# Where the tiles of a two-layer decoder trunk lie in on-chip memory: every large tile moved to a multiple of 512 bytes

## The chip, the cores and the metric

The kernel runs on one core of a Trainium2 chip. The metric is device time in microseconds for one execution, the median of several runs. The profile shown is of one execution of its own.

## The reference

The kernel computes a two-layer trunk on 512 tokens of width 1024, in float32. Cut to what matters:

```python
for i in range(2):
    if i == 0: mix = ssd_mixer(h, ...)        # in_proj, causal conv, chunked scan, gate, out_proj
    else:      mix = mla_attention(h, ...)    # low-rank q, shared compressed k/v, softmax, out_proj
    h = layer_norm(DN_ALPHA * h + mix, ln_mix_g[i], ln_mix_b[i])
    u = causal_depthwise_conv(h @ ffn_up[i], ffn_conv_w[i], ffn_conv_b[i])    # 1024 -> 2 x 2816
    g, val = split(u)
    h = layer_norm(DN_ALPHA * h + (silu(g) * val) @ ffn_down[i], ln_ffn_g[i], ln_ffn_b[i])
    if i == 0: shared_kv = mla_shared_kv(h, ...)
```

## The kernel before

**Arithmetic.** Every large product is done three times over in the fast float32 matmul format (float32r). Each operand is split into a high part, rounded to that format, and the rest, the low part; the product is high by high, plus low by high, plus high by low. Two helpers issue them. `mm_a` (the matmul is L123) keeps a 128x128 piece of a weight tile in the array (`wh` is its high part, `wl` its low part) and streams 512 (sometimes 256) columns of a transposed activation tile past it, `ht` in most places and `cT` in the attention's head projections. `mm_b` (L129, L130, L131) does it the other way round: a 128x128 piece of an activation tile stays in the array (`gt` in the FFN's down projection, `yT` in the SSD output projection, `oT` in the attention output projection, `cT` and `ht` in the attention's first projections), and 512 columns of `wh` or `wl` stream. What stays is the stationary operand, loaded by its own LDWEIGHTS instruction; what streams is the moving operand. Each matmul has a load of its own.

**Weights.** `WStream` brings weight pieces of 128x1024 from memory by DMA on SyncE's queue into `wst` (3 buffers). ScalarE rounds them into `wh` (L60), VectorE subtracts into `wl` (L61), 6 buffers each.

**Stages.** They follow each other: `ssd` (to about 433 us), `ffn` with its up projection, convolution and down projection (to about 790 us), `mla` (to about 985 us), and `ffn` again, whose last row block ends in `ln_last`. Within a stage TensorE, VectorE and ScalarE work side by side, in the order in which the program is written.

**Where tiles lie.** Tiles come from pools. A pool takes its place in on-chip memory behind the pools opened before it that are still open, each tile's size rounded up to 32 bytes; a tile has the same byte address in all 128 partitions. Pools of the class `K` live throughout; those of a stage are closed with it, and the next stage uses the same bytes. Some 1 KiB of tiles of a few bytes or a few hundred bytes (`mhalf`, `posi`, `freq`, `posf` in the pool `const`, `lnst` and `lnlast` in `lns`, `cw4`, `rstd`, `ng`, `hb` at the front of the SSD's pool, `css` and `smx` in `a2` ahead of the pool of `oT`) stand between or ahead of the large ones and shift all that come behind. So the large tiles lie at odd places. The remainder of each large tile's address by 512 in the built program:

| tiles | what they are | remainder before |
|---|---|---|
| `wst`, `wh`, `wl`, `ht`, `h`, `lngb` | weights, transposed activations (also V in the attention), residual, norm gains | 352 |
| `gt`, `acc`, `cw` | FFN | 32 |
| `yT`, `cv`, `th`, `W`, `y` and the other SSD tiles | SSD | 160 |
| `cT`, `ka`, `kb`, `qT`, `kT`, `qrT`, `PT`, `E` | attention | 32 |
| `oT` | attention output | 224 |
| `warm`, `ident` | constants | 128 |

All slices that a matmul takes of these tiles step by whole multiples of 512 bytes, but for the 288-column pieces of the SSD's first projection (steps of 128) and one of the attention's first projection (a step of 256).

Of the kernel before, what the change touches and what calls it, by code (L numbers as in the profile page):

```python
# [9 lines left out]
F32 = mybir.dt.float32  # L10
F32R = mybir.dt.float32r
BF16 = mybir.dt.bfloat16
I32 = mybir.dt.int32
# [5 lines left out]
P = 128  # L19
SEQ = 512  # L20
NT = SEQ // P
# [9 lines left out]
class WStream:  # L31
    def __init__(self, k, items, nb, nst, la):
        self.k, self.items, self.nb, self.nst, self.la = k, items, nb, nst, la
        self.loaded = 0
        self.split = 0
        self.done = 0
        self.st = {}
        self.w = {}
# [44 lines left out]
class K:  # L83
    def __init__(self, tc, ctx, nb=6, nst=3, la=4):
        self.tc, self.nc, self.ctx = tc, tc.nc, ctx
        nc = self.nc
        self.nb, self.nst, self.la = nb, nst, la
        pool = lambda n, b, **kw: ctx.enter_context(tc.tile_pool(name=n, bufs=b, **kw))
        self.const = pool("const", 1)
        self.hp = pool("hp", 1)  # L90
        self.htp = pool("htp", 1)
        self.wst = pool("wst", nst)
        self.wh = pool("wh", nb)
        self.wl = pool("wl", nb)
        self.lnp = pool("lnp", 1)
        self.lns = pool("lns", 2)
        self.ps = pool("ps", 8, space=PSUM)
        self.warm = self.const.tile([P, P], F32, name="warm")
        nc.vector.memset(self.warm, 1.0)
        self.ident = self.const.tile([P, P], F32, name="ident")  # L100
        make_identity(nc, self.ident)
        self.mhalf = self.const.tile([P, 1], F32, name="mhalf")
        nc.gpsimd.memset(self.mhalf, -0.5)
        self.h = self.hp.tile([P, NT, DM], F32, name="h")
        self.pend = []
        self.st = {}
# [32 lines left out]
    def add_mix(self, i, hf, ps, scale, last=False):  # L139


        hs = self.h[:, i, hf * 512:(hf + 1) * 512]
        kw = {}
        if last:
            if i not in self.st:
                self.st[i] = self.lns.tile([P, 6], F32, name="lnst", bufs=4)
            kw["accum_out"] = self.st[i][:, hf:hf + 1]
        a, b = (hs, ps) if isinstance(scale, float) else (ps, hs)
        self.nc.vector.scalar_tensor_tensor(hs, a, scale, b, op0=ALU.mult, op1=ALU.add, **kw)  # L149
# [18 lines left out]
    def ln_last(self, i, bs, out):  # L168

        nc = self.nc
        hv = self.h[:, i, :]
        s = self.st.pop(i)
        t = self.lns.tile([P, 12], F32, name="lnlast", bufs=1)
        c, qa, qb, sb, nmu, d, q, v, e, rstd, sa = (t[:, j:j + 1] for j in range(11))
        junk = self.junk[0].tile([P, DM], BF16, name="lnjunk", tag=self.junk[1])
        h2, h3 = hv[:, 512:768], hv[:, 768:]
        nc.vector.scalar_tensor_tensor(h2, h2, 1.0, bs[0], op0=ALU.mult, op1=ALU.add, accum_out=sa)
        nc.vector.tensor_scalar(sa, sa, s[:, 0:1], None, op0=ALU.add)  # L180
        nc.vector.tensor_scalar(c, sa, -1.0 / 768, None, op0=ALU.mult)
        nc.scalar.activation(junk[:, :768], hv[:, :768], AF.Square, bias=c, accum_out=qa)
        nc.vector.scalar_tensor_tensor(h3, h3, 1.0, bs[1], op0=ALU.mult, op1=ALU.add, accum_out=sb)
        nc.vector.tensor_scalar(nmu, sb, sa, -1.0 / DM, op0=ALU.add, op1=ALU.mult)
        nc.scalar.activation(junk[:, 768:], h3, AF.Square, bias=c, accum_out=qb)
        nc.vector.tensor_scalar(d, nmu, c, None, op0=ALU.subtract)
        nc.gpsimd.tensor_scalar(q, qa, 1.0 / DM, LN_EPS, op0=ALU.mult, op1=ALU.add)
        nc.vector.tensor_scalar(e, d, d, q, op0=ALU.mult, op1=ALU.subtract)
        for sl in (slice(0, 512), slice(512, 1024)):
            nc.vector.scalar_tensor_tensor(hv[:, sl], hv[:, sl], nmu, self.gb[:, 0, sl], op0=ALU.add, op1=ALU.mult)  # L190
        nc.gpsimd.tensor_scalar(v, qb, 1.0 / DM, e, op0=ALU.mult, op1=ALU.subtract)
        nc.gpsimd.tensor_tensor(rstd, v, self.mhalf, op=ALU.pow)
        for sl in (slice(0, 512), slice(512, 768), slice(768, 1024)):
            nc.vector.scalar_tensor_tensor(hv[:, sl], hv[:, sl], rstd, self.gb[:, 1, sl], op0=ALU.mult, op1=ALU.add)
            nc.sync.dma_start(out[:, sl], hv[:, sl])
# [153 lines left out]
NH, HD, NG, HPG, NS = 32, 64, 8, 4, 128  # L349
# [27 lines left out]
def ssd(k, ws, base, xT, x, cwp, hv, ngp, gb):  # L377
    nc, tc = k.nc, k.tc
    with ExitStack() as cx:
        pool = lambda n, b, **kw: cx.enter_context(tc.tile_pool(name=n, bufs=b, **kw))  # L380
        one = pool("s1", 1)
        cvp = pool("cv", 8)
        thp = pool("th", 2)
        k.junk = (thp, "th")
        ytp = pool("yt", 7)
        drp = pool("drp", 1, space=DRAM)


        cw = one.tile([P, 32, 5], F32, name="cw4")
        rstd = one.tile([P, NG, NT], F32, name="rstd")  # L390
        ng = one.tile([P, 2, 16], F32, name="ng")
        hb = one.tile([P, 2, NH], F32, name="hb")
        ht = k.new_ht()
        tri = one.tile([P, P], F32, name="tri")
        nc.gpsimd.memset(tri, 1.0)
# [408 lines left out]
def rope_tables(k, pos, freq):  # L804

    nc = k.nc
    c = k.const
    N = NT * 32
    pi = c.tile([P, NT], I32, name="posi")
    nc.sync.dma_start(pi, pos)  # L810
    fr = c.tile([P, 32], F32, name="freq")
    nc.sync.dma_start(fr, freq.broadcast_to([P, 32]))
    pf = c.tile([P, NT], F32, name="posf")
    nc.vector.tensor_copy(pf, pi)
    cs = c.tile([P, 2, NT, 32], F32, name="cossin")
    t = c.tile([P, 2, N], F32, name="ropet")
    a, m = t[:, 0], t[:, 1]
    v = lambda x: x.rearrange("p (c f) -> p c f", c=NT)
    nc.vector.tensor_tensor(v(a), pf.unsqueeze(2).broadcast_to([P, NT, 32]), fr.unsqueeze(1).broadcast_to([P, NT, 32]), op=ALU.mult)
    nc.vector.tensor_scalar(m, a, float(1.0 / (2.0 * np.pi)), ROUND, op0=ALU.mult, op1=ALU.add)  # L820
    nc.vector.tensor_scalar(m, m, ROUND, None, op0=ALU.subtract)
    for w in (TWO_PI_HI, TWO_PI_MID, TWO_PI_LO):
        nc.vector.scalar_tensor_tensor(a, m, -float(w), a, op0=ALU.mult, op1=ALU.add)
    lim = float(np.float32(3.1415925))
    sn = cs[:, 1].rearrange("p c f -> p (c f)")
    co = cs[:, 0].rearrange("p c f -> p (c f)")
    nc.vector.tensor_scalar(sn, a, lim, -lim, op0=ALU.min, op1=ALU.max)
    nc.vector.tensor_scalar(co, a, float(np.pi / 2), None, op0=ALU.add)
    nc.vector.tensor_scalar(m, co, float(np.pi), -2.0 * float(np.pi), op0=ALU.is_gt, op1=ALU.mult)
    nc.vector.tensor_tensor(co, co, m, op=ALU.add)  # L830
    nc.vector.tensor_scalar(co, co, lim, -lim, op0=ALU.min, op1=ALU.max)
    csf = cs.rearrange("p a c f -> p (a c f)")
    nc.scalar.activation(csf, csf, AF.Sin)
    k.cs = cs
# [18 lines left out]
def mla(k, ws, base, ngp, gb):  # L853
    nc, tc = k.nc, k.tc
    with ExitStack() as cx:
        pool = lambda n, b, **kw: cx.enter_context(tc.tile_pool(name=n, bufs=b, **kw))
        one = pool("a1", 1)
        two = pool("a2", 2)
        otp = pool("ot", 7)
        k.junk = (one, "E3")  # L860
        ng = one.tile([P, QR + KVR], F32, name="ang", tag="E3")
        nc.sync.dma_start(ng, ngp.broadcast_to([P, QR + KVR]))
# [246 lines left out]
def trunk_kernel(tc, *aps):  # L1109
    d = dict(zip(_INS, aps))  # L1110
    out = aps[len(_INS)]
    with ExitStack() as ctx:
        ctx.enter_context(tc.manual_schedule(engines={mybir.EngineType.SP}))
        k = K(tc, ctx)
        items = ssd_items(d['xbc'], d['zdt'], d['zw'], d['sow'])
        items += ffn_items(d['up'][0], d['down'][0])
        items += mla_items(d['dw'], d['vw'], d['rw'], d['hw'], d['aow'])
        items += ffn_items(d['up'][1], d['down'][1])
        ws = WStream(k, items, k.nb, k.nst, k.la)
        n = ssd(k, ws, 0, d['xT'], d['x'], d['cw4'], d['hv'], d['sng'], d['gb'][0])  # L1120
        rope_tables(k, d['pos'], d['freq'])
        n = ffn(k, ws, n, d['cw3'][0], d['gb'][1], la=5)
        n = mla(k, ws, n, d['ang'], d['gb'][2])
        n = ffn(k, ws, n, d['cw3'][1], d['gb'][3], out=out)
# [53 lines left out]
```

## Time and profile before

| what | value |
|---|---|
| median of 3 runs | 1360.01 us (1358.56 to 1360.58) |
| the profiled execution's own time | 1358.62 us |
| its span, first to last instruction | 1356.9 us |
| granted TensorE clock, share of full speed | 0.998 |
| TensorE matmul (PE) busy | 1341.7 us, 99% of the span |
| weight loads (PEld), overlapping PE | 1127.2 us, 83% |
| VectorE (DVE), ScalarE (ACT), GpSimd (POOL) busy | 885.6, 585.6, 71.5 us |
| mean traffic with memory | 100 GB/s |

In the profile PE is the matmul and PEld the weight load. A matmul's recorded duration holds its way through the array too, so that matmuls which follow each other overlap in the record: what one costs is the distance from its start to the next one's start. That distance is called the pace below. It is read from the timeline, which gives start times, or from the chain of work, which gives the length of an unbroken run of matmuls and their count.

### The profile page before, as it was taken

To read this page: it belongs to the slowest core of one execution; us is meant where nothing else is said; L and a number is where in the kernel's file an instruction comes from. 1 tells how busy PE (TensorE), PEld (TensorE's weight loads), DVE (VectorE), ACT (ScalarE), POOL (GpSimd) and SP (SyncE) were. 2 spreads that over 40 slices of the span, in tenths; PEclk is the share of its full clock that TensorE was granted. 3 is DMA by queue.
4 is the path that set the end of the run, shared out by engine and by line. 5 is a ranking of instruction groups with operands and counts; after the bars stand their busy time and mean duration, and the time that the engine had idled before them with its cause. 6 is when DMAs were issued, how large, how long until landed. Compare 5 with 4: busy or idle time off the path is not lost.

```text
span 1356.9 us, 17211 instructions
## 1 busy us (share of the span) xinstructions
PE 1341.7 (99%) x6819; PEld 1127.2 (83%) x6819; DVE 885.6 (65%) x1355; ACT 585.6 (43%) x927; POOL 71.5 (5%) x73
## 2 busy tenths in 40 slices
PE   9999999999999999999999999999999999999997
PEld 8878888888888888888888889888898888888886
DVE  7888778778788765425565366998576553465534
ACT  5765536526523544323443134665254431344421
POOL 0111101001102000000000021000100000000001
PEclk9999999999999999999999999999999999999999
DMA  7432332323232433232322222211052322323211
GB/s 240 179 118 95 108 120 82 109 100 103 96 106 64 143 102 100 85 101 95 106 95 85 85 88 65 92 48 63 31 189 93 98 96 89 106 94 102 91 55 63
DMA packets 44433, 135.14 MB, mean 100 GB/s; under 512 B 4768, under 2 KB 5792, under 8 KB 42816
## 3 DMA queue, kind: packets, MB, share of 16 engines
q1 hardware_dynamic: 44352, 134.04, 30.2%
q8 instruction: 53, 0.87, 0.3%
q14 instruction: 28, 0.23, 0.1%
HBM read 131.86 MB, written 2.16 MB: 99 GB/s over the span
## 4 chain that ended last, share of the span: by engine, by line
PE 91%; DVE 5%; DMA 2%; ACT 1%; issue 1%; POOL 0%; SPq 0%; POOLq 0%; DVEq 0%; ACTq 0%
PE ps L123 54%; PE ps L129 9%; PE ps L130 9%; PE ps L131 9%; PE ps L996 2%; PE ps L579 1%; PE ps L1031 1%; DVE wl L61 1%; PE ps L587 1%; PE ps L568 1%; DMA wst<-in_hw_dram 1%; PE ps L1018 1%; PE ps L680 1%; PE ps L205 1%; PE ps L525 0%
## 5 line engine op out<-in xcount | busy, mean ns | idle before, releaser
L123 PE MATMUL ps<-ht,wh 128*128 128x512 f32 (+1 forms) x2272 | 520.2, 379 | 0.8 <-ACT ht L208 0.8
L123 PEld LDWEIGHTS ps<-ht,wh 128*128 128x128 f32 x2272 | 408.4, 188 | 79.8 <-issue 1.2
L61 DVE TENSOR_TENSOR wl<-wst,wh 128x1024 fp32r<-128x1024 f32 (+3 forms) x226 | 273.9, 1217 | 155.9 <-ACT wh L60 155.6
L60 ACT CAST wh<-wst 128x1024 fp32r<-128x1024 f32 (+3 forms) x226 | 228.0, 1014 | 225.7 <-PE ps L131 171.0
L123 PE MATMUL ps<-ht,wl 128*128 128x512 f32 (+1 forms) x1136 | 267.2, 377 | 0.0
L123 PEld LDWEIGHTS ps<-ht,wl 128*128 128x128 f32 x1136 | 205.8, 188 | 39.5
L130 PE MATMUL ps<-wl,gt 128*128 128x512 f32 (+1 forms) x363 | 140.5, 387 | 0.0
L129 PE MATMUL ps<-wh,gt 128*128 128x512 f32 (+1 forms) x363 | 140.1, 386 | 0.0
L131 PE MATMUL ps<-wh,gt 128*128 128x512 f32 (+1 forms) x363 | 138.6, 382 | 0.0
L240 DVE SCALAR_TENSOR_TENSOR acc<-ps,cw,acc 128x511 f32<-128x511 f32 x88 | 65.5, 747 | 99.5 <-ACT acc L239 99.5
L440 DVE SCALAR_TENSOR_TENSOR cv<-ps,cw,cv 128x511 f32<-128x511 f32 (+2 forms) x96 | 71.5, 746 | 28.6 <-ACT cv L438 27.9
L239 ACT ACTIVATE acc<-ps,cw 128x512 f32<-128x512 f32 x88 | 68.4, 778 | 40.2 <-PE ps L123 40.2
L129 PEld LDWEIGHTS ps<-wh,gt 128*128 128x128 f32 x363 | 68.1, 188 | 14.9
L131 PEld LDWEIGHTS ps<-wh,gt 128*128 128x128 f32 x363 | 68.1, 188 | 14.4
L130 PEld LDWEIGHTS ps<-wl,gt 128*128 128x128 f32 x363 | 68.3, 188 | 12.8
L246 ACT CAST gt<-acc 128x512 fp32r<-128x512 f32 x44 | 27.3, 621 | 98.9 <-DVE acc L245 98.9
L149 DVE SCALAR_TENSOR_TENSOR h<-h,ps 128x512 f32<-128x512 f32 x47 | 31.2, 684 | 56.7 <-PE ps L131 56.7
L241 DVE SCALAR_TENSOR_TENSOR acc<-ps,cw,acc 128x510 f32<-128x510 f32 x88 | 65.7, 748 | 2.8
L244 ACT ACTIVATE acc<-acc 128x512 f32<-128x512 f32 x44 | 27.8, 632 | 87.0 <-DVE acc L241 86.9
L149 DVE SCALAR_TENSOR_TENSOR h<-ps,rstd,h 128x512 f32<-128x512 f32 x64 | 46.3, 749 | 21.9 <-PE ps L131 21.3
L159 POOL TENSOR_SCALAR lnst<-lnst 128x1 f32<-128x1 f32 x15 | 11.9, 796 | 870.7 <-ACT lnjunk L158 870.7
L129 PE MATMUL ps<-wh,yT 128*128 128x512 f32 x128 | 51.8, 405 | 0.0
(227 smaller groups left out, 1549.8 us busy)
## 6 DMA issues: line engine op xcount, KB each, us to landing
wst<-in_up_dram SPq DMA_DIRECT2D x88, 512.0 KB, 3.4
wst<-in_down_dram SPq DMA_DIRECT2D x40, 512.0 KB, 3.6
wst<-in_xbc_dram SPq DMA_DIRECT2D x32, 512.0 KB, 3.7
W<-cumd SPq DMA_DIRECT2D x8, 1024.0 KB, 4.6
wst<-in_sow_dram SPq DMA_DIRECT2D x16, 512.0 KB, 3.6
wst<-in_zw_dram SPq DMA_DIRECT2D x14, 512.0 KB, 3.5
lngb<-in_gb_dram SPq DMA_DIRECT2D x4, 1024.0 KB, 6.0
wst<-in_aow_dram SPq DMA_DIRECT2D x8, 512.0 KB, 3.4
```

The source lines that it names most:

```text
L60: nc.scalar.copy(h[:, :f], s[:, :f])
L61: nc.vector.tensor_tensor(l[:, :f], s[:, :f], h[:, :f], op=ALU.subtract)
L123: nc.tensor.matmul(out, w[:, k, :], xts[k][:, x, ts], start=first and p == 0 and k == 0, stop=last and p == 2 and k == nk - 1, skip_group_ ...
L129: nc.tensor.matmul(out, xt[:, 0, tsl], wh, start=start, stop=False, skip_group_check=True)
L130: nc.tensor.matmul(out, xt[:, 0, tsl], wl, start=False, stop=False, skip_group_check=True)
L131: nc.tensor.matmul(out, xt[:, 1, tsl], wh, start=False, stop=stop, skip_group_check=True)
L149: self.nc.vector.scalar_tensor_tensor(hs, a, scale, b, op0=ALU.mult, op1=ALU.add, **kw)
L239: nc.scalar.activation(a, b, AF.Identity, bias=cw[:, ch, 3:4], scale=cw[:, ch, 2:3])
L240: nc.vector.scalar_tensor_tensor(a[:, 1:], b[:, :SEQ - 1], cw[:, ch, 1:2], a[:, 1:], op0=ALU.mult, op1=ALU.add)
L241: nc.vector.scalar_tensor_tensor(a[:, 2:], b[:, :SEQ - 2], cw[:, ch, 0:1], a[:, 2:], op0=ALU.mult, op1=ALU.add)
L244: nc.scalar.activation(ag, ag, AF.Silu)
L440: nc.vector.scalar_tensor_tensor(t[:, d:], b[:, :SEQ - d], cw[:, ch, 3 - d:4 - d], t[:, d:], op0=ALU.mult, op1=ALU.add)
```

## The change

The tiles of a few bytes move to one pool `small`, opened first, that takes 384 bytes: `mhalf`, the four `lnst`, `lnlast`, `posi`, `freq`, `posf`. `lnlast` shrinks from 12 to 6 columns, and `ln_last` keeps its other five intermediate values in columns 1 to 5 of the row block's own `lnst` tile, in which only column 0 is still read by then. The SSD's four parameter tiles move to a pool `s0` behind the large ones, and the attention's pool `a2` (`css`, `smx`) behind that of `oT`.

```diff
+        self.small = pool("small", 1)
         self.const = pool("const", 1)
...
-        self.lns = pool("lns", 2)
...
-        self.mhalf = self.const.tile([P, 1], F32, name="mhalf")
+        self.mhalf = self.small.tile([P, 1], F32, name="mhalf")
...
-                self.st[i] = self.lns.tile([P, 6], F32, name="lnst", bufs=4)
+                self.st[i] = self.small.tile([P, 6], F32, name="lnst", bufs=4)
...
-        t = self.lns.tile([P, 12], F32, name="lnlast", bufs=1)
-        c, qa, qb, sb, nmu, d, q, v, e, rstd, sa = (t[:, j:j + 1] for j in range(11))
+        t = self.small.tile([P, 6], F32, name="lnlast")
+        c, qa, qb, sb, nmu, sa = (t[:, j:j + 1] for j in range(6))
+        d, q, v, e, rstd = (s[:, j:j + 1] for j in range(1, 6))
...
         ytp = pool("yt", 7)
+
+        par = pool("s0", 1)
...
-        cw = one.tile([P, 32, 5], F32, name="cw4")
-        rstd = one.tile([P, NG, NT], F32, name="rstd")
-        ng = one.tile([P, 2, 16], F32, name="ng")
-        hb = one.tile([P, 2, NH], F32, name="hb")
+        cw = par.tile([P, 32, 5], F32, name="cw4")
+        rstd = par.tile([P, NG, NT], F32, name="rstd")
+        ng = par.tile([P, 2, 16], F32, name="ng")
+        hb = par.tile([P, 2, NH], F32, name="hb")
...
-    pi = c.tile([P, NT], I32, name="posi")
+    pi = k.small.tile([P, NT], I32, name="posi")
...
-    fr = c.tile([P, 32], F32, name="freq")
+    fr = k.small.tile([P, 32], F32, name="freq")
...
-    pf = c.tile([P, NT], F32, name="posf")
+    pf = k.small.tile([P, NT], F32, name="posf")
...
         one = pool("a1", 1)
+        otp = pool("ot", 7)
         two = pool("a2", 2)
-        otp = pool("ot", 7)
```

After it the remainder by 512 is 0 for every tile of the table above. Their order in memory stays, and the shift is small: `ht` goes from byte 36192 to 36352, `wh` from 81248 to 81408, `gt` from 146976 to 146944, `yT` from 200352 to 199168, `oT` from 200416 to 200192.

No engine's instructions change their place, number or shape. The program differs in addresses, in the tile that five one-column operations of `ln_last` write, and in four waits that follow from which old tile lay under a new one: the first FFN's load of `cw` waits for ScalarE alone (before for TensorE, ScalarE and GpSimd), and the attention's fill of `cmask`, its first `css` operation and one matmul with `gt` wait for a slightly different set of old transfers and engines.

## Prediction

> **What bounds the kernel now.** I read the page's busy times and chain first, to see which engine sets the end.
>
> ```profile
> PE 1341.7 (99%) x6819; PEld 1127.2 (83%) x6819; DVE 885.6 (65%) x1355; ACT 585.6 (43%) x927; POOL 71.5 (5%) x73
> PE 91%; DVE 5%; DMA 2%; ACT 1%; issue 1%; POOL 0%; SPq 0%; POOLq 0%; DVEq 0%; ACTq 0%
> L61 DVE TENSOR_TENSOR wl<-wst,wh 128x1024 fp32r<-128x1024 f32 (+3 forms) x226 | 273.9, 1217 | 155.9 <-ACT wh L60 155.6
> L60 ACT CAST wh<-wst 128x1024 fp32r<-128x1024 f32 (+3 forms) x226 | 228.0, 1014 | 225.7 <-PE ps L131 171.0
> ```
>
> TensorE has work for 99% of the span and carries 91% of the chain that ended last. The other engines wait for it: ScalarE's weight rounding stood idle 171.0 us for L131's matmuls to give a buffer back, and VectorE's subtraction 155.6 us for ScalarE. A change of addresses can move the time by more than a little only if it changes the pace of matmuls.
>
> So I read the pace. Three runs in the chain of waits, in order of time (start, length, count), are pure `mm_a`:
>
> ```profile
> 617.84 119.68 PE ps L123 x528
> 986.37 8.64 PE ps L123 x72
> 1168.64 119.68 PE ps L123 x528
> ```
>
> The runs of 528 stream 512 columns each: 119.68 / 528 = 226.7 ns. The run of 72 streams 256 each: 8.64 / 72 = 120.0 ns. The 256 extra columns cost 106.7 ns, so 512 cost 213.3, and 13.3 ns are a fixed price per matmul, whatever its width.
>
> Is that price the same for other tiles? The timeline gives starts (start, duration, operation). For `gt`, `yT` and `oT` as the stationary operand, and `cT` as the moving one, these are the first and the last row of an unbroken row of matmuls of one kind (each a row of its own, left out here):
>
> ```profile
> 571.21 0.39 PE L130 MATMUL ps<-wl,gt 128*128 128x512 f32 x1
> ...
> 573.04 0.39 PE L129 MATMUL ps<-wh,gt 128*128 128x512 f32 x1
> ...
> 401.42 0.39 PE L129 MATMUL ps<-wh,yT 128*128 128x512 f32 x1
> ...
> 403.05 0.40 PE L130 MATMUL ps<-wl,yT 128*128 128x512 f32 x1
> ...
> 951.74 0.40 PE L130 MATMUL ps<-wl,oT 128*128 128x512 f32 x1
> ...
> 953.83 0.39 PE L130 MATMUL ps<-wl,oT 128*128 128x512 f32 x1
> ...
> 863.48 0.86 PE L123 MATMUL ps<-cT,wl 128*128 128x512 f32 x3
> 864.17 1.33 PE L123 MATMUL ps<-cT,wh 128*128 128x512 f32 x5
> 865.34 0.63 PE L123 MATMUL ps<-cT,wl 128*128 128x512 f32 x2
> 865.81 0.63 PE L123 MATMUL ps<-cT,wh 128*128 128x512 f32 x2
> ```
>
> `gt`: 8 matmuls in 1.83 us, 228.8 ns. `yT`: 7 in 1.63 us, 232.9. `oT`: 9 in 2.09 us, 232.2. `cT`: 10 in 2.33 us, 233.0. All stream 512 columns in the same format, yet the fixed price runs from 13.3 to 19.7 ns. `cT` and `ht` go through the same line L123 past the same `wh` and `wl`, `gt` and `yT` through the same L129 to L131: what differs is the tile, and with it the address.
>
> Take the moving operand's remainder minus the stationary one's, modulo 256. `ht` past `wh`: 352 - 352 = 0, 226.7 ns. `gt`: 352 - 32, 64, 228.8. `oT`: 352 - 224, 128, 232.2. `yT`: 352 - 160, 192, 232.9. `cT`: 32 - 352, also 192, 233.0. The two pairs at distance 192 share a pace though their remainders have nothing in common, and the pair at distance 0 is the fastest. [...]
>
> [...]
>
> **The change part by part.** After the change every such distance is 0 modulo 256. If distance decides, each group takes the pace of `ht`. The counts are these:
>
> ```profile
> L129 PE MATMUL ps<-wh,gt 128*128 128x512 f32 x341 | 133.9, 393 | 0.0
> L129 PE MATMUL ps<-wh,yT 128*128 128x512 f32 x128 | 51.8, 405 | 0.0
> L129 PE MATMUL ps<-wh,oT 128*128 128x512 f32 x64 | 25.6, 401 | 0.0
> L123 PE MATMUL ps<-cT,wh 128*128 128x512 f32 x80 | 23.1, 401 | 0.0
> L123 PE MATMUL ps<-cT,wl 128*128 128x512 f32 x40 | 11.9, 394 | 0.0
> L123 PE MATMUL ps<-ht,wh 128*128 128x512 f32 x2016 | 486.1, 391 | 0.0
> L123 PE MATMUL ps<-ht,wl 128*128 128x512 f32 x1008 | 249.0, 389 | 0.0
> ```
>
> L130 and L131 have as many as L129. So `gt`: 3 x 341 = 1023 matmuls, 2.1 ns each, 2.1 us. `yT`: 384 by 6.2 ns, 2.4 us. `oT`: 192 by 5.5 ns, 1.1 us. `cT` moving: 120 by 6.3 ns, 0.8 us. `cT` as stationary (distance 64) and the probabilities past V (32 - 352, 192) are a few dozen each; at the same gains I give them 0.4 us together. `ht` past `wh` and `wl`, more than half of all, keeps its distance of 0 and gains nothing. The sum is 6.8 us.
>
> All of it lies on TensorE, and I count it in full if TensorE stays the last one. One place is tight, and the table by stretches shows it against the two FFN ones:
>
> ```profile
> 620.00:735.00 115.00, 115.00 (x509) 95.24 (x508) 67.96 (x83) 48.76 (x62) 0.00 (x0) 1.00 0.29 96
> 560.00:600.00 40.00, 40.00 (x176) 32.85 (x175) 12.27 (x15) 8.57 (x9) 0.00 (x0) 1.00 0.31 99
> 399.00:412.00 13.00, 13.00 (x58) 10.46 (x57) 12.31 (x18) 4.39 (x6) 0.00 (x0) 1.00 0.25 80
> ```
>
> The columns are stretch, length, then busy time of PE, PEld, DVE, ACT, POOL. Late in the SSD output projection VectorE is busy 12.31 of 13.00 us; a faster TensorE could wait for it there. Some 100 of the `yT` matmuls stand there: at worst 0.6 us of their gain is lost. In the FFN VectorE and ScalarE have room.
>
> The rest I cost at nothing. The four changed waits: the first FFN's `cw` load is a transfer that nobody was seen waiting for, and the matmuls around it fill TensorE for longer than it lands. `ln_last` issues the same operations in the same order on one-column tiles; a tail of one-column operations with another base address can be neither a cost nor a gain that I could show. VectorE and ScalarE read and write tiles that shared a remainder already (`wst`, `wh`, `wl`, `h` at 352), so their distances stay 0. The DMA engines were busy 0.25 to 0.31 in these stretches, and landing sooner would hide behind the matmuls.
>
> The profiled execution took 1358.62 us, 1.4 below the median shown. 1358.62 - 6.8 = 1351.8; set against the median, **1353.2 us**. With 0.6 lost, or with the few slower matmuls after each change of tile also settling, this case spans 1350 to 1356.
>
> **The rivals.** *The absolute place costs too.* All remainders before are odd multiples of 32, so none of these tiles started on a multiple of 64, and the trace cannot show what such a start gives. [...] The rows bound it: the price cannot fall below 0. There are about 3024 + 384 (256-column ones) `ht` matmuls in L123, 1023 `gt`, and some 1300 others, 5700 in all; if half the price went, 6.7 ns x 5700 = 38 us, to 1315; if only a fifth, 2.7 ns, 15 us, to 1338. For it: the price is far from nothing. Against it, another place with distance 0 modulo 256: in the attention's first projection `ht` at 352 is stationary and a slice of `wh` or `wl` at 96 streams 320 columns.
>
> ```profile
> 809.63 0.31 PE L129 MATMUL ps<-wh,ht 128*128 128x320 f32 x1
> ...
> 810.07 0.34 PE L129 MATMUL ps<-wh,ht 128*128 128x384 f32 x1
> ```
>
> Three matmuls in 0.44 us are 146.7 ns; 320 columns cost 133.3 at the rate found above, and 13.3 ns are left again: moving one side by 256 bytes did nothing.
> [...]
>
> *Slower: zero is a bad place.* `ht` past `wh` holds the best pace of all those seen, in more than half of the matmuls, and the shift moves it as well. If low distance was not the reason, and its new place has the pace of another group, 3024 matmuls lose. At the pace of `gt` for everything: 3024 x 2.1 = +6.4 for `ht`, `yT` -1.6, `oT` -0.7, `cT` -0.5: +3.6, to 1363.6. At the pace of `yT` for everything: 3024 x 6.2 = +18.7 and `gt` +4.2, to 1383. It decides from the point where `ht` loses 6.8 us / 3024 = 2.2 ns. For it: any move from the best pace is likelier to lose than to gain, if nothing explains it. Against it: distance explains all five groups. That all engines now meet at one remainder is no reason: in the stretch 620 to 735, `wst`, `wh`, `wl`, `ht` lay at one remainder, VectorE was busy 67.96 of 115 us on such tiles, and the matmuls kept 226.7 ns throughout.
>
> *Nothing happens.* The paces belong to the pattern of accesses (how often the stationary or moving slice repeats), not to addresses; all stay, and the time is 1360. For it: `yT` and `oT` change slices otherwise than `ht`. Against it: `gt` and `yT` have the same pattern and differ by 4 ns.
>
> **How the numbers follow.** Distance decides: 0.57. The absolute place helps on top: 0.13. Zero is a bad place: 0.21. Nothing: 0.09. About 0.2%, 2.7 us, is what measurements of this kernel can tell from no change. Faster by more: 0.57 + 0.13 = 0.70; same 0.09; slower 0.21. The range runs from the near end of the second case, 1338, to a little above the near end of the third, 1366; that leaves out the larger halves of both, near 0.2 together. The likeliest case's own range is 1350 to 1356.
>
> **What would show it.** In the profile after, the chain's runs x528 should again be 119.7 us long, and the timeline's pace with `gt`, `yT`, `oT` and `cT` should fall to 226.7 ns. If x528 is shorter, the absolute place matters: 118.0 per run would be a quarter of the price. If it is longer than 120.9 (2.2 ns each), the third case holds and I am wrong in sign. If the paces with `yT` and `cT` still read 233, distance was not the reason.

## The result, and the profile after

| | before | after |
|---|---|---|
| median | 1359.83 us (1358.56 to 1360.8, 6 runs) | 1354.55 us (1353.97 to 1356.25, 6 runs) |
| profiled execution, its span | 1358.62, 1356.9 us | 1354.52, 1352.8 us |

The ratio of the medians is 0.9962, with a 95% interval of 0.9952 to 0.9973: 5.3 us faster, 3.7 to 6.5. The forecast was 1353.2 us. The lines of after stand 1 to 4 lower in the program: L123 is now L124, L129 to L131 are L130 to L132, L568 and L579 are L572 and L583.

The page of after, busy times and the group of the rounding:

```profile
PE 1337.5 (99%) x6819; PEld 1127.6 (83%) x6819; DVE 885.4 (65%) x1355; ACT 585.5 (43%) x927; POOL 71.4 (5%) x73
L60 ACT CAST wh<-wst 128x1024 fp32r<-128x1024 f32 (+3 forms) x226 | 227.9, 1013 | 223.6 <-PE ps L132 168.5
```

PE is busy 1337.5 us where it was 1341.7; the other engines did the same work in the same time, and ScalarE still waits for TensorE to give buffers back. So the time came from TensorE itself. The three runs of `ht` past `wh` and `wl` in after's chain:

```profile
616.72 119.68 PE ps L124 x528
983.30 8.63 PE ps L124 x72
1164.98 119.68 PE ps L124 x528
```

Their pace has not moved: 226.7 ns for 512 columns, 119.9 for 256. The others' did. From after's timeline, the first and the last of unbroken rows of matmuls of one kind, for `gt` and, close behind a change of tile and later, for `oT`; then `cT`:

```profile
569.64 0.39 PE L130 MATMUL ps<-wh,gt 128*128 128x512 f32 x1
...
572.36 0.39 PE L130 MATMUL ps<-wh,gt 128*128 128x512 f32 x1
...
948.05 0.40 PE L131 MATMUL ps<-wl,oT 128*128 128x512 f32 x1
...
948.97 0.39 PE L132 MATMUL ps<-wh,oT 128*128 128x512 f32 x1
...
951.69 0.39 PE L132 MATMUL ps<-wh,oT 128*128 128x512 f32 x1
...
861.74 0.85 PE L124 MATMUL ps<-cT,wl 128*128 128x512 f32 x3
862.43 1.32 PE L124 MATMUL ps<-cT,wh 128*128 128x512 f32 x5
863.58 0.62 PE L124 MATMUL ps<-cT,wl 128*128 128x512 f32 x2
864.03 0.62 PE L124 MATMUL ps<-cT,wh 128*128 128x512 f32 x2
```

`gt`: 12 matmuls in 2.72 us, 226.7 ns (228.8 before). `oT`: 4 in 0.92 us, 230, just after the change of tile, and then 12 in 2.72, 226.7 (232.2 before). `cT`: 10 in 2.29 us, 229.0 (233.0 before), or 229.9 by the trace's own times, which are not rounded to 0.01 us; these runs have 15 matmuls each, and no settled pace is seen in them. With `yT` it is as with `oT`: 15 matmuls from 401.39 to 404.79 us, 226.7 (232.9 before).

Summed over the matmuls of the two traces, paired one to one, as the distance from each start to the next one's (the rows of `gt` and of `cT` stationary hold the 512-column matmuls alone):

| group | forecast, us | saved, us |
|---|---|---|
| `gt` | 2.1 | 2.37 |
| `yT` | 2.4 | 1.96 |
| `oT` | 1.1 | 0.94 |
| `cT` moving | 0.8 | 0.45 |
| `cT` stationary, probabilities past V | 0.4 | 0.27 |
| `ht` moving | 0 | -0.36 |
| SSD's first projection, L680 | not costed | 0.76 |
| 100 to 105 us, L568 and L579 | not costed | -1.62 |

Six matmuls of the SSD's first projection, between 5.3 and 6.8 us, hold 0.65 of its 0.76 us: they went at 240 ns each in before and at 130 to 135 in after. `gt` has 66 matmuls of 256 columns too, and those lost 0.14 us (117.8 ns before, 119.9 after). With the small pieces left out here all pairs add up to 4.04 us.

The last row is a surprise. The same stretch by windows (its columns as in the prediction's, then the granted clock, DMA share and GB/s), before, then after, and then the first matmuls in it from each timeline:

```profile
96.00:106.00 10.00, 7.03 (x59) 5.83 (x59) 9.19 (x16) 3.23 (x5) 1.04 (x1) 1.00 0.38 118
```

```profile
96.00:106.00 10.00, 7.00 (x52) 5.69 (x50) 8.95 (x16) 3.24 (x5) 1.04 (x1) 0.83 0.32 102
```

```profile
100.86 1.56 PE L568 MATMUL ps<-wx,bk 128*128 128x256 f32 x6 [2.98 <-DVE wx L561]
```

```profile
100.18 2.31 PE L572 MATMUL ps<-wx,bk 128*128 128x256 f32 x6 [3.00 <-DVE wx L565]
```

TensorE waits 3 us for `wx` in both, but after it the granted clock over these 10 us is 0.83 in after and 1.00 in before, and six matmuls take 2.31 us for 1.56. Whether that is the change is asked below.

### The profile page after: what moved, and what is told of

Same layout as the page of the kernel before. It is cut to its first block, busy times and chain, and to the rows that moved or that the text cites. A ratio compares the mean times of both kernels' runs of the same rounds, so it can differ in the third digit from the quotient of the medians.

```text
span 1352.8 us, 17212 instructions
## 1 busy us (share of the span) xinstructions
PE 1337.5 (99%) x6819; PEld 1127.6 (83%) x6819; DVE 885.4 (65%) x1355; ACT 585.5 (43%) x927; POOL 71.4 (5%) x73
## 4 chain that ended last, share of the span: by engine, by line
PE 91%; DVE 5%; DMA 1%; ACT 1%; issue 1%; POOL 0%; SPq 0%; POOLq 0%; DVEq 0%; ACTq 0%
PE ps L124 54%; PE ps L130 9%; PE ps L131 9%; PE ps L132 9%; PE ps L1000 2%; PE ps L583 1%; PE ps L1035 1%; DVE wl L61 1%; PE ps L591 1%; PE ps L572 1%; PE ps L1022 1%; PE ps L684 1%; PE ps L207 1%; PE ps L529 0%; PE ps L554 0%
## 5 line engine op out<-in xcount | busy, mean ns | idle before, releaser
L124 PE MATMUL ps<-ht,wh 128*128 128x512 f32 (+1 forms) x2272 | 520.5, 379 | 1.2 <-ACT ht L210 1.2
L124 PEld LDWEIGHTS ps<-ht,wh 128*128 128x128 f32 x2272 | 408.3, 188 | 80.3 <-ACT ht L210 1.4
L124 PE MATMUL ps<-ht,wl 128*128 128x512 f32 (+1 forms) x1136 | 267.2, 377 | 0.0
L124 PEld LDWEIGHTS ps<-ht,wl 128*128 128x128 f32 x1136 | 205.8, 188 | 39.6
L130 PE MATMUL ps<-wh,gt 128*128 128x512 f32 (+1 forms) x363 | 139.1, 383 | 0.0
L132 PE MATMUL ps<-wh,gt 128*128 128x512 f32 (+1 forms) x363 | 138.9, 383 | 0.0
L131 PE MATMUL ps<-wl,gt 128*128 128x512 f32 (+1 forms) x363 | 138.9, 383 | 0.0
L132 PEld LDWEIGHTS ps<-wh,gt 128*128 128x128 f32 x363 | 68.2, 188 | 13.4
L131 PEld LDWEIGHTS ps<-wl,gt 128*128 128x128 f32 x363 | 68.2, 188 | 13.3
L130 PEld LDWEIGHTS ps<-wh,gt 128*128 128x128 f32 x363 | 68.2, 188 | 13.2
L130 PE MATMUL ps<-wh,yT 128*128 128x512 f32 x128 | 51.3, 401 | 0.0
```

The lines of the kernel that those rows point to most:

```text
L124: nc.tensor.matmul(out, w[:, k, :], xts[k][:, x, ts], start=first and p == 0 and k == 0, stop=last and p == 2 and k == nk - 1, skip_group_ ...
L130: nc.tensor.matmul(out, xt[:, 0, tsl], wh, start=start, stop=False, skip_group_check=True)
L131: nc.tensor.matmul(out, xt[:, 0, tsl], wl, start=False, stop=False, skip_group_check=True)
L132: nc.tensor.matmul(out, xt[:, 1, tsl], wh, start=False, stop=stop, skip_group_check=True)
```

## The experiments

All are edits of the kernel after. The theory under test: the start of the moving operand minus that of the stationary one, modulo 256 bytes, called the distance, sets a matmul's pace. Paces are read as above, from the chain or from the first and last row of an unbroken row of matmuls. In the rows below a 512-column matmul is recorded at 0.39 to 0.40 us, while the next one starts 0.227 to 0.234 us after it on average; what the rest of the record holds no run shows.

### Everything shifted together by 32 bytes (shift_all_32)

```diff
         self.small = pool("small", 1)
+        self.small.tile([P, 8], F32, name="shift")
```

> All tiles of the changed kernel move up together by 32 bytes, so that every large tile lies at 32 modulo 512 and every distance between moving and stationary operand stays 0. Theory (distance decides): paces as in the changed kernel, 226.7 ns with ht, gt, yT, oT and cT, time about 1354.5 us. Rival (the multiple of 64 or 512 bytes itself matters): the runs of 528 matmuls leave 119.68 us, and the time leaves 1354.5 us by over 3 us. Rival (the change gained by something else, such as the other waits or the moved parameter tiles): also 1354.5 us, but then the next kernels don't react to distances.

1355.2 us (1354.61 to 1355.84), ratio to before 0.9967, interval 0.9956 to 0.9979: the time of after. Its chain:

```profile
617.51 119.68 PE ps L125 x528
...
1165.44 119.68 PE ps L125 x528
```

With every large tile at 32 beyond a multiple of 512, the pace is 226.7 ns again, as it was at 352 and at 0. The same holds with `gt`: its 512-column matmuls in the second FFN average 226.7 ns here and in after. So what counted in these runs is not that the tiles lie at multiples of 512, but that they lie alike.

### `ht` 64 bytes below the weights (ht_64_below_weights)

```diff
         self.htp = pool("htp", 1)
+        pool("gap", 1).tile([P, 16], F32, name="gap")
```

> 64 unused bytes between ht and the weight tiles in the changed kernel: ht past wh and wl gets distance 0 - 64, that is 192 modulo 256; gt, yT, oT and cT move along with wh and wl and keep 0; in the attention's first projection wh past ht gets 64. Theory (distance decides): ht past wh and wl goes from 226.7 to 233 ns, 3024 x 6.3 = 19 us more, and with some for the 256-column ones 1373 to 1376 us; gt, yT and oT stay at 226.7 ns. Rival (ht's pace is due to its access pattern): 226.7 ns stays and the time is 1354.5 us.

1371.29 us (1369.32 to 1372.26), ratio 1.0083, interval 1.0066 to 1.0099. Its chain:

```profile
625.00 123.20 PE ps L125 x528
...
994.66 8.18 PE ps L125 x72
1178.51 123.20 PE ps L125 x528
```

123.20 / 528 = 233.3 ns: 64 bytes between two tiles, with no instruction moved, cost 6.7 ns a matmul in these runs. Paired with after's, the 3024 matmuls lost 18.8 us. The 256-column matmuls went the other way, 8.18 / 72 = 113.6 ns for 119.9 in this run and 114 to 117 on average over each of the three places where they stand; the 384 of them gave 1.8 us back. Expected were 1373 to 1376 us, so less was lost than that. The distance 192 cost 6.7 ns with 512 columns and saved up to 6.3 with 256.

### Every distance of `gt`, two in each run

```diff
-        pools = {"fw": pool("fw", 4), "gt": pool("gt", 12), "cw": pool("cw", 1)}
+        pools = {"fw": pool("fw", 4)}
+        if gpad:
+            pool("gpad", 1).tile([P, gpad // 4], F32, name="gpad")
+        pools.update(gt=pool("gt", 12), cw=pool("cw", 1))
```

The two FFNs get a `gpad` each, which moves `gt` up and leaves a distance of 256 - `gpad`. First 64 and 128 (gt_64_and_128):

> Only gt moves, by 64 bytes in the first FFN (distance 192 modulo 256) and by 128 in the second (distance 128). Theory (distance decides): the pace of the matmuls with gt is 233 ns in the first FFN and 232 in the second, against 226.7 in both in the changed kernel; the time is 512 x 6.3 + 512 x 5.5 = 6 us more, about 1360.5 us. Rival (pace belongs to the tile's access pattern or to any odd address): both FFNs alike, at 226.7 or at 228.8 ns.

Its timeline, the first and last of an unbroken row in the first and in the second FFN:

```profile
570.66 0.39 PE L132 MATMUL ps<-wh,gt 128*128 128x512 f32 x1
...
581.86 0.39 PE L132 MATMUL ps<-wh,gt 128*128 128x512 f32 x1
...
1119.73 0.39 PE L130 MATMUL ps<-wh,gt 128*128 128x512 f32 x1
...
1130.88 0.40 PE L130 MATMUL ps<-wh,gt 128*128 128x512 f32 x1
```

48 matmuls in 11.20 us, 233.3 ns, at distance 192; 48 in 11.15, 232.3, at 128. The run took 1360.27 us. Then 192 and 256 (gt_192_and_256):

> Only gt moves, by 192 bytes in the first FFN (distance 64 modulo 256) and by 256 in the second (distance 0 modulo 256, 256 modulo 512). Theory (distance modulo 256 decides): 228.8 ns in the first FFN as in the kernel before, 226.7 in the second; time 512 x 2.1 = 1.1 us more, about 1355.6 us. Rival (512 is the period): the second FFN leaves 226.7 ns.

The same view:

```profile
570.63 0.39 PE L132 MATMUL ps<-wh,gt 128*128 128x512 f32 x1
...
581.84 0.39 PE L130 MATMUL ps<-wh,gt 128*128 128x512 f32 x1
...
1119.64 0.39 PE L132 MATMUL ps<-wh,gt 128*128 128x512 f32 x1
...
1130.97 0.39 PE L131 MATMUL ps<-wl,gt 128*128 128x512 f32 x1
```

49 in 11.21 us, 228.8 ns, at distance 64: the pace that `gt` had before at that distance. 50 in 11.33, 226.6, at 256, the pace of distance 0: 512 bytes are not the period. 1357.12 us in one run. Then the values between (gt_32_and_96, gt_160_and_224):

> Only gt moves, by 32 bytes in the first FFN (distance 224 modulo 256) and by 96 in the second (distance 160). The measured paces so far are 226.7 ns at 0, 228.9 at 64, 232.4 at 128, 233.3 at 192. Theory that the pace follows the distance smoothly: between 128 and 192, that is about 233 ns, in the second FFN; in the first either over 233 (it goes on rising) or between 233.3 and 226.7 (it falls back to 0). Rival (only whole steps of 64 bytes count): 233.3 ns in the first FFN as at 192, 232.4 in the second as at 128. Time about 1361 us.

In its timeline:

```profile
570.65 0.40 PE L132 MATMUL ps<-wh,gt 128*128 128x512 f32 x1
...
581.86 0.40 PE L132 MATMUL ps<-wh,gt 128*128 128x512 f32 x1
...
1119.77 0.39 PE L131 MATMUL ps<-wl,gt 128*128 128x512 f32 x1
...
1130.78 0.40 PE L130 MATMUL ps<-wh,gt 128*128 128x512 f32 x1
```

> Only gt moves, by 160 bytes in the first FFN (distance 96 modulo 256) and by 224 in the second (distance 32). Smooth theory: between 228.9 and 232.4 ns in the first FFN, about 227.8 in the second. Steps of 64: 228.9 and 226.7 ns. If any distance has a pace under 226.7 ns, there is a better place than 0. Time 1355 to 1358 us.

And in the other's:

```profile
570.79 0.39 PE L132 MATMUL ps<-wh,gt 128*128 128x512 f32 x1
...
581.99 0.39 PE L132 MATMUL ps<-wh,gt 128*128 128x512 f32 x1
...
1119.62 0.40 PE L131 MATMUL ps<-wl,gt 128*128 128x512 f32 x1
...
1130.82 0.40 PE L131 MATMUL ps<-wl,gt 128*128 128x512 f32 x1
```

233.5 ns at distance 224 (48 in 11.21 us), 234.3 at 160 (47 in 11.01); 233.3 at 96 and 233.3 at 32 (48 in 11.20 both). These took 1361.41 and 1360.8 us in one run each, the second well above the 1355 to 1358 expected. A smooth rise with distance is refuted, and so are whole steps of 64 bytes: 32 bytes off already cost 6.6 ns, as much as 192 bytes do. Zero is a good place (226.7 ns), 64 a half-good one (228.8), and all others tried at steps of 32 are alike, 232.3 to 234.3.

### 16 and 4 bytes off (gt_16_and_4)

```diff
-                gt = pools["gt"].tile([P, 2, SEQ], F32R, name="gt")
+                gt = view(pools["gt"].tile([P, 2 * SEQ + 128], F32R, name="gt"))
...
-        n = ffn(k, ws, n, d['cw3'][0], d['gb'][1], la=5)
+        n = ffn(k, ws, n, d['cw3'][0], d['gb'][1], la=5, view=lambda t: t[:, 4:4 + 2 * SEQ].rearrange("p (a s) -> p a s", a=2))
...
-        n = ffn(k, ws, n, d['cw3'][1], d['gb'][3], out=out)
+        n = ffn(k, ws, n, d['cw3'][1], d['gb'][3], out=out, view=lambda t: t[:, 1:1 + 2 * SEQ].rearrange("p (a s) -> p a s", a=2))
```

> gt lies in wider buffers at a multiple of 512; in the first FFN its values start 16 bytes into them (distance 240 modulo 256), in the second 4 bytes (252). So far the paces are 226.7 ns at 0, 229 at 64, and 232 to 234 at 32, 96, 128, 160, 192 and 224. Theory (0 is a single good place, and what is not a multiple of 64 away from it pays in full): 233 ns in both FFNs. Rival (a distance under some line size counts as 0): 226.7 ns at 4, or at both.

Its timeline, first and second FFN:

```profile
570.75 0.39 PE L130 MATMUL ps<-wh,gt 128*128 128x512 f32 x1
...
581.86 0.39 PE L131 MATMUL ps<-wl,gt 128*128 128x512 f32 x1
...
1119.68 0.39 PE L131 MATMUL ps<-wl,gt 128*128 128x512 f32 x1
...
1130.83 0.40 PE L131 MATMUL ps<-wl,gt 128*128 128x512 f32 x1
```

16 bytes cost nothing: 49 matmuls in 11.11 us, 226.7 ns. 4 bytes do: 48 in 11.15, 232.3. 1357.77 us in one run. So neither expectation held. The good place is not the one value 0; a tile 16 bytes off is still in it, and one 4 or 32 bytes off is not. Why 4 and 32 bytes cost when 16 don't, no run shows.

### High and low part of `gt` at different distances (gt_hi_lo)

```diff
-        n = ffn(k, ws, n, d['cw3'][0], d['gb'][1], la=5)
+        n = ffn(k, ws, n, d['cw3'][0], d['gb'][1], la=5, view=lambda t: t[:, :2 * (SEQ + 8)].rearrange("p (a s) -> p a s", a=2)[:, :, :SEQ])
...
-        n = ffn(k, ws, n, d['cw3'][1], d['gb'][3], out=out)
+        n = ffn(k, ws, n, d['cw3'][1], d['gb'][3], out=out, view=lambda t: t[:, 8:8 + 2 * (SEQ + 56)].rearrange("p (a s) -> p a s", a=2)[:, :, :SEQ])
```

In the first FFN the high part lies at distance 0 and the low part at 224, in the second the other way round.

> The high and the low part of gt get distances of their own: in the first FFN high 0 and low 224, in the second high 224 and low 0 (224 costs 6.7 ns where both have it). Of three matmuls L130 and L131 use the high part and L132 the low one. Theory A (the running matmul meets the load of the next one's weights): first FFN, the matmul ahead of the low part's (L131) is the slow one of three; second FFN, L130 and L132 are slow and L131 is not. Theory B (a matmul's distance to its own stationary operand counts): first FFN L132 slow, second FFN L130 and L131 slow. Sum of three about 680 + 6.7 ns in the first FFN and 680 + 13.3 in the second under both.

Its timeline:

```profile
570.63 0.40 PE L130 MATMUL ps<-wh,gt 128*128 128x512 f32 x1
...
581.83 0.40 PE L130 MATMUL ps<-wh,gt 128*128 128x512 f32 x1
...
1119.76 0.40 PE L130 MATMUL ps<-wh,gt 128*128 128x512 f32 x1
...
1130.90 0.39 PE L130 MATMUL ps<-wh,gt 128*128 128x512 f32 x1
```

In the first FFN 16 rounds of three take 11.20 us, 700.0 ns a round, in the second 11.14, 696; after's round is 3 x 226.7 = 680. Expected were 687 and 693. In the first FFN one stationary part in three is at a bad distance, 224, and the round costs as much as with all three there (3 x 233.5). The price isn't a sum of one per matmul in this run. One run took 1362.03 us. The single matmuls don't settle it: in the first FFN L131 is the slowest on average (239 ns), as Theory A has it, but so it is in the first FFN of gt_160_and_224 (237), where all three lie at distance 96. Whether Theory A or B holds stays open.

### The old distances on the new layout (distances_back)

```diff
-        pools = {"fw": pool("fw", 4), "gt": pool("gt", 12), "cw": pool("cw", 1)}
+        pools = {"fw": pool("fw", 4)}
+        pool("pad", 1).tile([P, 48], F32, name="pad")
+        pools.update(gt=pool("gt", 12), cw=pool("cw", 1))
...
+        pool("pad", 1).tile([P, 16], F32, name="pad")
         one = pool("s1", 1)
...
+        pool("pad", 1).tile([P, 48], F32, name="pad")
         one = pool("a1", 1)
```

> The changed kernel with all its pools, waits and multiples of 64 bytes, but with unused bytes ahead of the FFN's gt (192), the SSD's tiles (64) and the attention's (192), so that the old distances return: gt 64, yT 192, cT moving 192 and stationary 64; only oT gets 64 instead of 128. Theory (the whole gain is distance): gt + 1023 x 2.2 = 2.3 us, yT + 384 x 5.5 = 2.1, cT + 120 x 4.1 = 0.5, oT + 192 x 1.9 = 0.4, probabilities past V 0.2: 5.5 us more than the changed kernel, about 1360 us, the time of the kernel before. Rival (other parts of the change, such as the waits and the moved parameter tiles, give a part): between 1354.5 and 1359 us.

1358.56 us (1357.74 to 1359.72, 11 runs) beside 1360.37 for before (15 runs); ratio 0.9989, interval 0.9980 to 0.9998. Its timeline, `yT` and `gt`:

```profile
401.71 0.40 PE L131 MATMUL ps<-wl,yT 128*128 128x512 f32 x1
...
411.98 0.40 PE L130 MATMUL ps<-wh,yT 128*128 128x512 f32 x1
...
570.68 0.39 PE L132 MATMUL ps<-wh,gt 128*128 128x512 f32 x1
...
581.89 0.39 PE L130 MATMUL ps<-wh,gt 128*128 128x512 f32 x1
```

The old paces are back: 44 in 10.27 us, 233.4, and 49 in 11.21, 228.8. From 0.9962 the ratio rose to 0.9989, 3.7 us of the 5.3, with the new pools and the new `ln_last` still in place. `oT` came to lie at distance 64 here, not at the old 128, and has 229.0 ns; 192 matmuls by 3.2 ns make 0.6 us of what is missing, and that alone would lie within the interval (0.3 to 2.7 us below before). Whether any of the other 1.2 us is real, and then due to the new pools or waits, these runs can't tell.

### Is the lower clock at 100 us part of the change? (fill_gap)

```diff
+                if g == 1:
+                    for _ in range(10):
+                        nc.tensor.matmul(pb[:, GC:GC + P], k.warm, k.warm, start=True, stop=True)
```

Ten matmuls whose result is not used stand in TensorE's wait for `wx`.

> The changed kernel with ten matmuls of constants (warm past itself, into a part of a bank that is overwritten afterwards) in the place near 97 us where TensorE waits 3.0 us for wx. In the profile after, the granted clock between 99 and 105 us is 0.72, and the matmuls there take 1.6 us longer than in the profile before, where it is 1.00. Theory (the idle stretch lowers the clock, and the shift of some 0.7 us of the program against the clock's own rhythm decides whether it does): clock 1.00 there, 1.6 us less, 1352.9 us. Rival (the slower matmuls there come from the new addresses of wx, bk, W and xdt): clock or not, the time stays at 1354.5 us.

1354.57 us (1352.65 to 1355.14), ratio 0.9964, interval 0.9950 to 0.9978. Its window, and the first matmuls after the wait:

```profile
96.00:106.00 10.00, 9.36 (x79) 8.09 (x78) 9.09 (x16) 3.24 (x5) 1.04 (x1) 1.00 0.46 127
```

```profile
100.68 1.56 PE L575 MATMUL ps<-wx,bk 128*128 128x256 f32 x6 [0.64 <-DVE wx L565]
```

The clock stays at 1.00 and the six matmuls take 1.56 us again, with `wx` and `bk` where they were. That agrees with the theory, in one profile; that the idle wait is what lowers the clock it does not show. The total did not fall with it, though; 1352.9 us had been expected. In the chains of the two profiles (fill_gap, then after):

```profile
152.49 16.59 PE ps L124 x72
...
806.02 7.32 DMA ang<-in_ang_dram
...
983.39 8.63 PE ps L124 x72
```

```profile
153.20 16.59 PE ps L124 x72
```

fill_gap came to these matmuls 0.5 us later than after (100.68 us for 100.18). It is 0.7 us ahead at 153 us, and 0.1 behind at 983 (after: 983.30); on the way its chain waits for a load of `ang`, which after's does not. Such waits differ between these two executions, and by 983 us the lead of 0.7 us is gone.

The window from 96 to 106 us has a clock of 0.68 to 0.84 in the ten profiles other than before's and fill_gap's, after's among them, and distances_back has 0.83 with the old distances. So the dip is not tied to the distances. A narrower window shows what it is made of, in after and in gt_192_and_256:

```profile
100.84:104.25 3.41, 3.41 (x23) 2.59 (x23) 3.22 (x7) 1.00 (x2) 1.04 (x1) 0.50 0.00 0
```

```profile
99.54:106.36 6.82, 5.33 (x30) 4.33 (x32) 5.88 (x11) 2.71 (x5) 1.04 (x1) 0.50 0.19 69
```

The clock is 0.50 for 3.41 us in eight of the ten profiles, and for twice as long in the other two (gt_192_and_256 and gt_hi_lo). In all ten the dip begins 95.57 us, 28 times a dip's 3.413, after the trace first records the full clock at the kernel's start. That record begins somewhere from 3.9 to 7.2 us, at 5.3 in after and at 6.8 in before. So in these traces the dips lie at whole multiples of 3.41 us from a start that differs in each execution. That the place of the wait against these steps decides whether the clock falls is an estimate from these figures, and no run shows it. The pace of the six early matmuls changes with the same record: in before they go at 240 ns up to the 6.8 us at which the full clock begins, and in after, where it begins at 5.3, at 130 to 135. TensorE's idle time alone does not tell when the clock falls: TensorE was busy for 1.91 us of the 3.41 ahead of the dip in gt_192_and_256, and for 1.53 us of the step from 98.99 to 102.40 in before, which no dip followed. Whether before has it in its other executions, of which no profile exists, is open too.

## Why the prediction was right, and where not

**The bound.** Right: the busy times of VectorE, ScalarE and GpSimd stayed within 0.2 us, PE's fell by 4.2 us.

**The reason.** Right that the distance between moving and stationary operand decides, with the place itself of no account at the three tried: the runs x528 kept 119.68 us at 352, 0 and 32, and grew to 123.20 when only the distance changed. The rival "the absolute place costs too" fell with shift_all_32. "Zero is a bad place" fell with the chain of after, and "nothing happens" with the paces. Why the distance sets the pace no run shows, and gt_hi_lo, which was to tell Theory A from Theory B, did not. The remainders were not all odd multiples of 32, as the prediction has it (`warm` and `ident` lay at 128); no term rests on that.

**How the price depends on it.** Not seen, though that did no harm here. The prediction had paces at four distances that happened to be 0, 64, 128 and 192, and they rise from 226.7 to 233.0 ns. Those at 32, 96, 160 and 224 show no slope: 233.3, 233.3, 234.3, 233.5 ns. Had the change brought tiles near to each other instead of exactly together, by 32 bytes say, a forecast along that rise would have been a gain, and the result, estimated from the paces of `gt`, a loss.

**The terms.** The five add up to 5.99 us where 6.8 was forecast. `gt`, with long runs, gave all of its term, less the 0.14 us of its 256-column matmuls, which were not costed. `yT`, `oT` and above all `cT` gave less, since the first matmuls after a change of tile still go at about 230 ns, and the forecast used the settled pace for all: 0.45 for 0.8 with `cT`, 1.96 for 2.4 with `yT`. The 0.6 us that VectorE was allowed to take was not seen as a wait of its own.

**Against its own profiled time** the forecast was 1351.8 us and after's profile took 1354.52. Of the 2.7 between, 0.8 are the terms, and 1.6 the stretch at 100 us, which no part of the prediction looked at: a wait of 3 us was counted as idle time alone, and the granted clock of 0.83 from 96 to 106 us (1.00 in before) is a missing term. The full clock, recorded from 5.3 us on for 6.8 in before, gave 0.65 back at the start. Nothing here ties either to the change. Set against the median the miss is 1.35 us, since before's profiled execution lay 1.2 below its own median of six. The forecast gain of 6.8 us lies a little above the measured interval, 3.7 to 6.5.

## What to carry to other kernels

Where TensorE is the bound and a weight load goes with each matmul, read the pace per pair of tiles: in these runs those of one shape, 512 columns, went at 226.7 to 234.3 ns by the places of their tiles in memory. For streams of 512 columns, put moving and stationary tiles so that their starts differ by a multiple of 256 bytes (226.7 ns here), which is done by collecting small tiles in one pool, and check it by shifting one tile. For 256 columns that was no good place in these runs (119.9 ns, and 113.6 at 192). The difference is 3% of a 512-column matmul here, 6.7 of 226.7 ns, so it is worth looking for after larger things. All of this was seen with float32r and a 128x128 weight load for each matmul, and with nothing else.

## What the runs showed that was not expected

- The good place is narrow: 16 bytes off cost nothing (226.7 ns), 4 and 32 bytes cost 5.6 and 6.6 ns.
- For 256 columns it is another place: with `ht` 113.6 ns at distance 192, 119.9 at 0; with `gt` 119.9 and 120.1 on average at 0 and 128, but 117.8 at 64, 117.4 at 160 and 116.7 at 32. The best place tried is not the same for the two lengths of stream.
- After a change of tile a few matmuls go at about 230 ns before the pace settles at 226.7, even at distance 0.
- Behind a wait of TensorE, of 2.5 us in ht_64_below_weights and 3.0 in the others, the granted clock fell in ten profiles (0.68 to 0.84 over 10 us) and in one not (1.00, before's); in after it cost 1.6 us. Narrower, it was 0.50 for 3.41 or 6.82 us, from a start that differs in each execution, and TensorE had been busy for 1.91 us of the 3.41 ahead of one of these dips.
